# Attention queries and keys transposed unsplit and split on the way out of PSUM

## The chip, the cores and the metric

The kernel runs on one core of a Trainium2 chip. A core has five engines with queues of their own: TensorE (PE in the profile; its weight loads are PEld), VectorE (DVE), ScalarE (ACT), GpSimd (POOL) and SyncE (SP), which issues the DMAs. An engine works through its queue in order; semaphores make one wait for another. The metric is device microseconds of one execution of the whole program.

## The reference

A trunk of two layers over 2048 tokens of width 1024 in float32: a Mamba-2 layer and a layer of sliding-window attention with sinks. The change concerns the second.

```python
def swa_sink_mixer(h, cos, sin, w_in, sinks, w_out):
    q, k, v, gate = jnp.split(h @ w_in, [ATT_WIDTH, ...], axis=-1)      # 16 heads of q, 4 of k and v, 64 wide
    q = apply_partial_rope(q.reshape(b, L, ATT_Q_HEADS, D), cos, sin)   # the first 16 of 64 columns rotate
    k = apply_partial_rope(k.reshape(b, L, Hk, D), cos, sin)
    s = jnp.einsum('bnikgd,bnjkd->bnkgij', qb, kb) * (D ** -0.5)        # blocks of 128 against 256 keys
    s = jnp.where(valid, s, -jnp.inf)                                   # window of 128
    m = jnp.maximum(jnp.max(s, axis=-1, keepdims=True), sink)
    p = jnp.exp(s - m)
    denom = jnp.sum(p, axis=-1, keepdims=True) + jnp.exp(sink - m)
    o = jnp.einsum('bnkgij,bnjkd->bnikgd', p / denom, vb)
    return (o.reshape(b, L, ATT_WIDTH) * jax.nn.silu(gate)) @ w_out
```

The whole layer is x + rmsnorm(mixer(rmsnorm(x))). Float32 products are made of three F32R matmuls each: an operand is rounded to F32R (hi) and its remainder is rounded too (lo), and hi*hi + hi*lo + lo*hi are summed in PSUM (`mm3`, lines 89 to 93).

## The kernel before

The attention layer is the function `att`. It runs a loop over n of 64 iterations: two halves of the tokens, in each of them four groups of heads (kv: four heads of q, one of k and v), in each of these eight blocks of 128 tokens (i). Three more iterations empty the pipeline. `hf`, `kv` and `i` are n // 32, n // 8 % 4 and n % 8.

In one iteration n, five blocks are in work at once. `proj(n)` makes q, k and v of block n with 24 matmuls (lines 91 to 93 with operands qh, ql) and, at its end, brings them out of the PSUM tile ps: the columns that don't rotate by ScalarE (line 362), v by VectorE (line 364), the rotation by VectorE (lines 371 to 374). The result is qf, four heads of q and one of k. `stage_a(n - 1)` transposes, `stage_b(n - 2)` makes scores and softmax (lines 422 to 442), `stage_c(n - 3)` transposes the probabilities (line 450) and masks them (lines 452 and 456), and, in each second iteration, `stage_d` multiplies two blocks with v (lines 471 and 475) and writes them out. An iteration with `stage_d` is longer than one without; they alternate. Between these parts stand pieces of `proj` and of `gate_mm`, which projects the gate (lines 91 to 93 with whi, wlo; lines 347 and 348).

Before the change, the split into hi and lo is made ahead of the transposes. ScalarE rounds q (line 376), GpSimd subtracts (line 377), so that hi and lo of a head stand side by side as 128 columns; VectorE does the same for k (lines 380 and 381), with hi twice and lo twice. One transpose per head of q then gives a tile with hi in partitions 0 to 63 and lo in 64 to 127; two transposes give k as hi over hi and lo over lo. The scores of a head are two matmuls over 128 partitions (line 422), which together sum all four products.

PSUM is scarce here. The pool `tp` has a single buffer (tag "tr"), which the tiles tq (transposed q), tt (transposed probabilities) and pt (transposed x) take in turn. The pool `pp` has four (tag "pj"): the ps of projections and gates, tk (transposed k), and the u of the output projection.

At i = 0 a group of heads begins: SyncE loads its weights, ScalarE rounds them (lines 151 and 331) and GpSimd subtracts (lines 153 and 333), in tiles wraw, whi, wlo (gate) and qr, qh, ql (q, k and v).

The program is written through a tile framework, which sets the order on each engine itself by a plan made ahead of the run, and adds the semaphores. The order therefore differs from that of the code, and it changes where an edit changes the plan.

Of the kernel before, what the change touches and what calls it, by code (L numbers as in the profile page):

```python
# [11 lines left out]
F32 = mybir.dt.float32  # L12
F32R = mybir.dt.float32r
I32 = mybir.dt.int32
U32 = mybir.dt.uint32
AF = mybir.ActivationFunctionType
ALU = mybir.AluOpType
# [4 lines left out]
P = 128  # L22
# [37 lines left out]
class Trunk:  # L60
# [7 lines left out]
    def consts(self, pool):  # L68
        nc = self.nc
        self.ident = pool.tile([P, P], F32, name="ident")  # L70
        make_identity(nc, self.ident)
        self.identr = pool.tile([P, P], F32R, name="identr")
        nc.vector.tensor_copy(self.identr, self.ident)
        self.ones = pool.tile([P, P], F32, name="ones")
        nc.gpsimd.memset(self.ones, 1.0)

        self.triu = pool.tile([P, P], F32, name="triu")
        nc.gpsimd.affine_select(self.triu, self.ones, pattern=[[1, P]], compare_op=ALU.is_ge,
                                fill=0.0, base=0, channel_multiplier=-1)
        self.mhalf = pool.tile([P, 1], F32, name="mhalf")  # L80
        nc.vector.memset(self.mhalf, -0.5)
# [214 lines left out]
    def att(self, ctx, x1, oT, wn, rs1, hs0, wout, sts):  # L296
        nc, io = self.nc, self.io
        w_in = io["att_w_in"][0]
        KO, VO, GO = QW, QW + KVW, QW + 2 * KVW
        if True:  # L300
            wp = self.pool(ctx, "c_w", 2)
            cp = self.pool(ctx, "c_c")
            ap = self.pool(ctx, "c_a", 2)
# [11 lines left out]
            ksave = [cp.tile([P, 2, P], F32R, name=f"ksave{n}") for n in range(4)]  # L315
            vsave = [cp.tile([P, 64], F32, name=f"vsave{n}") for n in range(4)]
            NS = 64
            S = [dict() for _ in range(NS)]
# [31 lines left out]
            def proj(n, ws, hs):  # L350
                hf, kv, i = n // 32, n // 8 % 4, n % 8
                hi, lo = hs[i // 4]
                sl = slice((i % 4) * P, (i % 4) * P + P)
                ps = self.pp.tile([P, 6, 64], F32, tag="pj", name="ps")
                pf = ps.rearrange("p a b -> p (a b)")
                for k in range(KD):
                    wh, wl = ws[k]
                    self.mm3(pf, hi[:, k, sl], lo[:, k, sl], wh, wl, k == 0, k == KD - 1)
                    if k % 2 == 1 and k < KD - 1:
                        yield 1.0  # L360
                qf = ap.tile([P, 5, 64], F32, tag="qf", name="qf")
                nc.scalar.activation(qf[:, :, 16:64], ps[:, 0:5, 16:64], AF.Copy)
                vt = vsave[kv] if (hf == 0 and i == 7) else ap.tile([P, 64], F32, tag="vt", name="vt", bufs=6)
                nc.vector.tensor_copy(vt, ps[:, 5, :])
                ti = 8 * hf + i
                m1 = ap.tile([P, 5, 16], F32, tag="m1", name="m1")
                m2 = ap.tile([P, 5, 16], F32, tag="m2", name="m2")

                def bc(t, a, b):
                    return t[:, ti, a:b].unsqueeze(1).to_broadcast([P, 5, b - a])  # L370
                nc.vector.tensor_tensor(m1, ps[:, 0:5, 0:16], bc(self.cs2, 0, 16), ALU.mult)
                nc.vector.tensor_tensor(m2[:, :, 0:8], ps[:, 0:5, 8:16], bc(self.sn2, 0, 8), ALU.mult)
                nc.vector.tensor_tensor(m2[:, :, 8:16], ps[:, 0:5, 0:8], bc(self.sn2, 8, 16), ALU.mult)
                nc.vector.tensor_tensor(qf[:, :, 0:16], m1, m2, ALU.add)
                qs = ap.tile([P, 4, 2, 64], F32R, tag="qs", name="qs")
                nc.scalar.activation(qs[:, :, 0, :], qf[:, 0:4, :], AF.Copy)  # L376
                nc.gpsimd.tensor_tensor(qs[:, :, 1, :], qf[:, 0:4, :], qs[:, :, 0, :].bitcast(F32), ALU.subtract)  # L377
                ks = ap.tile([P, 2, 2, 64], F32R, tag="ks", name="ks")
                kb = qf[:, 4:5, :].to_broadcast([P, 2, 64])
                nc.vector.tensor_copy(ks[:, 0, :, :], kb)  # L380
                nc.vector.tensor_tensor(ks[:, 1, :, :], kb, ks[:, 0, :, :].bitcast(F32), ALU.subtract)  # L381
                S[n].update(qs=qs, ks=ks, vt=vt)

            def stage_a(n):
                hf, kv, i = n // 32, n // 8 % 4, n % 8
                qs, ks = S[n]["qs"], S[n]["ks"]
                tq = self.tp.tile([P, 4, P], F32, tag="tr", name="tq")
                for r in range(4):
                    nc.tensor.transpose(tq[:, r, :].bitcast(F32R), qs[:, r].rearrange("p a b -> p (a b)"), self.identr)  # L389
                qT = ap.tile([P, 4, P], F32R, tag="qT", name="qT")  # L390
                nc.scalar.activation(qT, tq, AF.Copy)
                tk = self.pp.tile([P, 2, P], F32, tag="pj", name="tk")
                for v in range(2):
                    nc.tensor.transpose(tk[:, v, :].bitcast(F32R), ks[:, v].rearrange("p a b -> p (a b)"), self.identr)  # L394
                if i == 0:
                    kk = ap.tile([P, 2, 2 * P], F32R, tag="kk", name="kk", bufs=3)
                    if hf == 1:
                        nc.vector.tensor_copy(kk[:, :, 0:P], ksave[kv].bitcast(F32))
                    S[n]["kk"] = kk
                kk = S[n]["kk"]  # L400
                nc.vector.tensor_copy(kk[:, :, P:2 * P], tk)
                if i < 7:
                    k2 = ap.tile([P, 2, 2 * P], F32R, tag="kk", name="kk", bufs=3)
                    nc.scalar.activation(k2[:, :, 0:P], tk, AF.Copy)
                    S[n + 1]["kk"] = k2
                elif hf == 0:
                    nc.scalar.activation(ksave[kv], tk, AF.Copy)
                S[n]["qT"] = qT

            def stage_b(n):  # L410
# [79 lines left out]
            for n in range(NS + 3):  # L490
                pr = iter(())
                if n < NS:
                    hf, kv, i = n // 32, n // 8 % 4, n % 8
                    if n == 28:
                        hs2 = []
                        pre = self.prep(x1, 2, wn, hs2, rs1)
                        next(pre)
                    if 28 <= n < 32:
                        next(pre)
                    if n == 32:  # L500
                        drain(pre)
                        hs = hs2
                    if n % 32 == 0:
                        pre = self.prep(x1, 2 * hf + 1, wn, hs, rs1)
                        next(pre)
                    if i == 0:
                        wg = [self.split_w(w_in[:, GO + 256 * kv + P * c:GO + 256 * kv + P * c + P], P)
                              for c in range(2)]
                        ws = load_qkv(kv)
                    if i % 4 == 0:  # L510
                        drain(gate)
                        gate = gate_mm(kv, i // 4, hs, wg)
                        if n % 32 == 0:
                            drain(gate)
                    if n % 32 < 4:
                        next(pre)
                    pr = proj(n, ws, hs)
# [25 lines left out]
                if n % 2 == 0:  # L543
                    lagged(stage_d, n - 3)
                lagged(stage_a, n - 1)
                part(True)
            drain(head)
# [475 lines left out]
```

## Time and profile before

| | us |
|---|---|
| median of three runs (lowest, highest) | 2607.88 (2606.68, 2608.61) |
| the profiled execution | 2604.63 |
| its span, first to last instruction | 2602.9 |
| TensorE busy | 2555.3 |
| VectorE busy | 1726.8 |
| ScalarE busy | 1264.8 |
| GpSimd busy | 1087.6 |

The mean granted clock of TensorE over the span is 0.998 of full speed. The attention loop runs from about 1780 to 2430 us of the span. The profile names an instruction by engine, line, operation and tiles (out<-in). A matmul's time contains its way through the array, so that matmuls in a row overlap: their pace is read from their starts. "L364 DVE ... [0.34 <-ACT qf L362]" says that VectorE stood idle for 0.34 us ahead of this instruction until ScalarE's line 362 released it.

### The profile page before, as it was taken

Reading aid. Unit: us, or ns where it says so; the run is one execution under the profiler, and the core shown is the slowest. Engines: PE = TensorE matmul, PEld = TensorE weight load, DVE = VectorE, ACT = ScalarE, POOL = GpSimd, SP = SyncE. Lnnn points to the kernel's source line nnn. Section 1 sums busy time; section 2 is a strip of 40 time slices with the busy share of each in tenths; the row PEclk is TensorE's granted clock in tenths of the full one; section 3 lists DMA queues with packets and bytes.
Section 4 is the critical chain, followed back from the end, with each engine's and each line's share of the span. In section 5 each row is a group of like instructions: output and inputs, shape, how many; then the busy total and the mean of one; then the engine's idle time right before and its main releaser. Section 6 shows DMA issues by size and latency. Waiting matters only on the chain. (4 is left out here: it accounts for less than half of the span.)

```text
span 2602.9 us, 39510 instructions
## 1 busy us (share of the span) xinstructions
PE 2555.3 (98%) x14307; PEld 2128.2 (82%) x14307; DVE 1726.8 (66%) x3580; ACT 1264.8 (49%) x3015; POOL 1087.6 (42%) x1013
## 2 busy tenths in 40 slices
PE   7999999999999999999998999999999999999998
PEld 6778888888777888888886888888888888888787
DVE  6678666776787667766687544447777777777422
ACT  5455555555654555555556323324455455554321
POOL 2455555655555556555566322222222122221222
PEclk9999999999999999999999999999999999999999
DMA  4332222222323222222225332234111121101343
GB/s 126 104 81 70 82 76 75 84 64 82 100 73 116 74 78 80 71 78 78 78 81 152 117 104 91 96 131 143 54 53 54 57 79 53 54 27 61 110 146 122
DMA packets 266659, 224.50 MB, mean 86 GB/s; under 512 B 31136, under 2 KB 229984, under 8 KB 266464
## 3 DMA queue, kind: packets, MB, share of 16 engines
q1 hardware_dynamic: 266464, 221.98, 27.9%
q8 instruction: 113, 1.85, 0.3%
q14 instruction: 82, 0.67, 0.1%
HBM read 179.72 MB, written 42.21 MB: 85 GB/s over the span
## 5 line engine op out<-in xcount | busy, mean ns | idle before, releaser
L91 PE MATMUL ps<-hi,whi 128*128 128x512 f32 (+1 forms) x1808 | 732.2, 405 | 1.4 <-ACT hi L140 1.0
L93 PE MATMUL ps<-hi,wlo 128*128 128x512 f32 (+1 forms) x1808 | 707.3, 391 | 0.4 <-POOL wlo L153 0.4
L92 PE MATMUL ps<-lo,whi 128*128 128x512 f32 (+1 forms) x1808 | 703.7, 389 | 0.5 <-DVE lo L141 0.5
L91 PEld LDWEIGHTS ps<-hi,whi 128*128 128x128 f32 x1808 | 341.1, 189 | 77.9 <-issue 18.8
L93 PEld LDWEIGHTS ps<-hi,wlo 128*128 128x128 f32 x1808 | 340.8, 188 | 76.4 <-POOL wlo L153 1.2
L92 PEld LDWEIGHTS ps<-lo,whi 128*128 128x128 f32 x1808 | 342.0, 189 | 57.4 <-DVE lo L141 1.3
L745 DVE SCALAR_TENSOR_TENSOR acc<-raw,cw,acc 128x512 f32<-128x512 f32 x384 | 344.0, 896 | 21.7 <-ACT acc L742 17.2
L153 POOL TENSOR_TENSOR wlo<-wraw,whi 128x1024 fp32r<-128x1024 f32 x114 | 282.6, 2479 | 173.3 <-ACT whi L151 164.7
L798 ACT ACTIVATE dec<-ab,acs 128x128 f32<-128x128 f32 x512 | 167.1, 391 | 174.0 <-DMA ab<-atd 168.1
L804 POOL TENSOR_TENSOR ab<-ab,sx 128x512 f32<-128x512 f32 x120 | 163.2, 1360 | 193.2 <-ACT ab L803 193.0
L252 PE MATMUL u<-oh,yh 128*128 128x512 f32 x768 | 241.1, 394 | 0.0
L252 PE MATMUL u<-ol,yh 128*128 128x512 f32 x768 | 239.3, 392 | 0.0
L252 PE MATMUL u<-oh,yl 128*128 128x512 f32 x768 | 237.8, 390 | 0.0
L748 ACT ACTIVATE sx<-acc 128x512 f32<-128x512 f32 x128 | 80.8, 632 | 267.0 <-DVE acc L745 266.9
L377 POOL TENSOR_TENSOR qs<-qf,qs 128x256 fp32r<-128x256 f32 x64 | 48.7, 762 | 343.5 <-ACT qs L376 306.7
L236 POOL TENSOR_TENSOR yl<-yr,yh 128x1024 fp32r<-128x1024 f32 (+1 forms) x64 | 120.5, 1883 | 160.5 <-ACT yh L234 157.9
L841 POOL TENSOR_TENSOR ysb<-ysb,zz 128x128 f32<-128x128 f32 x256 | 162.6, 648 | 49.5 <-DVE ysb L839 48.7
L91 PE MATMUL ps<-qh,hi 128*128 128x384 f32 x512 | 177.8, 348 | 0.0
L92 PE MATMUL ps<-ql,hi 128*128 128x384 f32 x512 | 173.0, 338 | 0.9 <-POOL ql L333 0.9
L93 PE MATMUL ps<-qh,lo 128*128 128x384 f32 x512 | 172.2, 337 | 0.0
L252 PEld LDWEIGHTS u<-oh,yl 128*128 128x128 f32 x768 | 144.2, 188 | 31.8 <-issue 0.6
L252 PEld LDWEIGHTS u<-ol,yh 128*128 128x128 f32 x768 | 143.8, 188 | 30.7 <-issue 0.2
(217 smaller groups left out, 4759.6 us busy)
## 6 DMA issues: line engine op xcount, KB each, us to landing
wraw<-in_ssm_w_in SPq DMA_DIRECT2D x98, 512.0 KB, 3.9
ab<-atd SPq DMA_DIRECT2D x128, 256.0 KB, 3.3
xt<-in_x SPq DMA_DIRECT2D x32, 512.0 KB, 4.9
yT<-ysb SPq DMA_DIRECT2D x64, 256.0 KB, 2.2
yr<-yT SPq DMA_DIRECT2D x32, 512.0 KB, 4.0
xt<-x SPq DMA_DIRECT2D x32, 512.0 KB, 4.1
oraw<-in_ssm_w_out SPq DMA_DIRECT2D x16, 512.0 KB, 6.1
x<-xt SPq DMA_DIRECT2D x32, 256.0 KB, 2.1
```

Source lines behind the costliest of these rows:

```text
L91: nc.tensor.matmul(ps, sh, mh, start=first, stop=False)
L92: nc.tensor.matmul(ps, sh, ml, start=False, stop=False)
L93: nc.tensor.matmul(ps, sl, mh, start=False, stop=last)
L153: nc.gpsimd.tensor_tensor(lo, raw, hi.bitcast(F32), ALU.subtract)
L236: nc.gpsimd.tensor_tensor(yl, yr, yh.bitcast(F32), ALU.subtract)
L252: nc.tensor.matmul(st["u"][h], y[:, k, :], w[:, j, 512 * h:512 * h + 512], start=k0 + k == 0 and m == 0, stop=k0 + k == kt - 1 and m == 2)
L377: nc.gpsimd.tensor_tensor(qs[:, :, 1, :], qf[:, 0:4, :], qs[:, :, 0, :].bitcast(F32), ALU.subtract)
L745: nc.vector.scalar_tensor_tensor(acc, raw[:, j:j + BLK], self.cw[:, j, ct:ct + 1], acc, ALU.mult, ALU.add)
L748: nc.scalar.activation(sx, acc, AF.Tanh)
L798: nc.scalar.activation(dec[:, r, :], ab[:, r, :], AF.Relu, scale=-1.0, bias=acs[:, c, 4 * g + r:4 * g + r + 1])
L804: nc.gpsimd.tensor_tensor(ce, ce, Ct[:, sl].unsqueeze(1).to_broadcast([P, 4, P]), ALU.mult)
L841: nc.gpsimd.tensor_tensor(yv, yv, res[f"z{pr}", s][:, sl], ALU.mult)
```

## The change

q and k are transposed as they are, and split afterwards. Two heads of q make 128 columns of qf, so two transposes give all four heads; qf gets a sixth head, a copy of k, so that a third transpose gives k twice, in partitions 0 to 63 and 64 to 127. All three go into one tile tq of the pool `tp`, and are F32 now, with the F32 identity. Out of PSUM, for each of the two heads of a pair, ScalarE rounds its 64 partitions into hi, and VectorE subtracts into the other 64 partitions of qT (lines 388 and 389 afterwards). k is rounded over all 128 partitions and subtracted likewise (lines 396 and 397). The copy of k for the next block is made by GpSimd from SBUF (lines 400 and 403), instead of by ScalarE from PSUM. The tiles qs, ks, tk and the F32R identity go. The scores (line 422, afterwards 418) are untouched. Lines from `consts` to `proj` have numbers smaller by 2 afterwards, lines behind `stage_a` smaller by 4: line 450 becomes 446, line 442 becomes 438.

```diff
-        self.identr = pool.tile([P, P], F32R, name="identr")
-        nc.vector.tensor_copy(self.identr, self.ident)
...
-                qf = ap.tile([P, 5, 64], F32, tag="qf", name="qf")
-                nc.scalar.activation(qf[:, :, 16:64], ps[:, 0:5, 16:64], AF.Copy)
+                qf = ap.tile([P, 6, 64], F32, tag="qf", name="qf")
+                nc.scalar.activation(qf[:, 0:5, 16:64], ps[:, 0:5, 16:64], AF.Copy)
...
-                nc.vector.tensor_tensor(qf[:, :, 0:16], m1, m2, ALU.add)
-                qs = ap.tile([P, 4, 2, 64], F32R, tag="qs", name="qs")
-                nc.scalar.activation(qs[:, :, 0, :], qf[:, 0:4, :], AF.Copy)
-                nc.gpsimd.tensor_tensor(qs[:, :, 1, :], qf[:, 0:4, :], qs[:, :, 0, :].bitcast(F32), ALU.subtract)
-                ks = ap.tile([P, 2, 2, 64], F32R, tag="ks", name="ks")
-                kb = qf[:, 4:5, :].to_broadcast([P, 2, 64])
-                nc.vector.tensor_copy(ks[:, 0, :, :], kb)
-                nc.vector.tensor_tensor(ks[:, 1, :, :], kb, ks[:, 0, :, :].bitcast(F32), ALU.subtract)
-                S[n].update(qs=qs, ks=ks, vt=vt)
+                nc.vector.tensor_tensor(qf[:, 0:5, 0:16], m1, m2, ALU.add)
+                nc.vector.tensor_copy(qf[:, 5, :], qf[:, 4, :])
+                S[n].update(qf=qf, vt=vt)
 
             def stage_a(n):
                 hf, kv, i = n // 32, n // 8 % 4, n % 8
-                qs, ks = S[n]["qs"], S[n]["ks"]
-                tq = self.tp.tile([P, 4, P], F32, tag="tr", name="tq")
-                for r in range(4):
-                    nc.tensor.transpose(tq[:, r, :].bitcast(F32R), qs[:, r].rearrange("p a b -> p (a b)"), self.identr)
+                qf = S[n]["qf"].rearrange("p a b -> p (a b)")
+                tq = self.tp.tile([P, 3, P], F32, tag="tr", name="tq")
+                for t in range(3):
+                    nc.tensor.transpose(tq[:, t, :], qf[:, t * P:(t + 1) * P], self.ident)
                 qT = ap.tile([P, 4, P], F32R, tag="qT", name="qT")
-                nc.scalar.activation(qT, tq, AF.Copy)
-                tk = self.pp.tile([P, 2, P], F32, tag="pj", name="tk")
-                for v in range(2):
-                    nc.tensor.transpose(tk[:, v, :].bitcast(F32R), ks[:, v].rearrange("p a b -> p (a b)"), self.identr)
+                qe = qT.rearrange("p (t e) i -> p e t i", e=2)
+                for e in range(2):
+                    rows, other = slice(64 * e, 64 * e + 64), slice(64 - 64 * e, P - 64 * e)
+                    nc.scalar.activation(qe[rows, e], tq[rows, 0:2, :], AF.Copy)
+                    nc.vector.tensor_tensor(qe[other, e], tq[rows, 0:2, :], qe[rows, e].bitcast(F32), ALU.subtract)
...
                 kk = S[n]["kk"]
-                nc.vector.tensor_copy(kk[:, :, P:2 * P], tk)
+                nc.scalar.activation(kk[:, 0, P:2 * P], tq[:, 2, :], AF.Copy)
+                nc.vector.tensor_tensor(kk[:, 1, P:2 * P], tq[:, 2, :], kk[:, 0, P:2 * P].bitcast(F32), ALU.subtract)
                 if i < 7:
                     k2 = ap.tile([P, 2, 2 * P], F32R, tag="kk", name="kk", bufs=3)
-                    nc.scalar.activation(k2[:, :, 0:P], tk, AF.Copy)
+                    nc.gpsimd.tensor_copy(k2[:, :, 0:P], kk[:, :, P:2 * P].bitcast(F32))
                     S[n + 1]["kk"] = k2
                 elif hf == 0:
-                    nc.scalar.activation(ksave[kv], tk, AF.Copy)
+                    nc.gpsimd.tensor_copy(ksave[kv], kk[:, :, P:2 * P].bitcast(F32))
```

The plan moves with it. TensorE's queue at the start of the loop, where n = 1 begins: before,

```order
L91 MATMUL ps<-qh,hi 128x384
L92 MATMUL ps<-ql,hi 128x384
L93 MATMUL ps<-qh,lo 128x384
L394 MATMUL tk<-identr,ks 128x128
L137 MATMUL pt<-ident,xt 128x128 x3
L389 MATMUL tq<-identr,qs 128x128 x4
L394 MATMUL tk<-identr,ks 128x128
L137 MATMUL pt<-ident,xt 128x128
```

and now, with lines 135 and 383 for the transposes of x and of qf:

```order
L89 MATMUL ps<-qh,hi 128x384
L90 MATMUL ps<-ql,hi 128x384
L91 MATMUL ps<-qh,lo 128x384
L135 MATMUL pt<-ident,xt 128x128 x4
L89 MATMUL ps<-qh,hi 128x384
L90 MATMUL ps<-ql,hi 128x384
L91 MATMUL ps<-qh,lo 128x384
L89 MATMUL ps<-qh,hi 128x384
L90 MATMUL ps<-ql,hi 128x384
L91 MATMUL ps<-qh,lo 128x384
L89 MATMUL ps<-qh,hi 128x384
L90 MATMUL ps<-ql,hi 128x384
```

The first transposes of the loop have moved behind the transposes of x and nine projection matmuls.

VectorE's queue in a short iteration of the second half of the tokens, from the sum of the row maxima on: before,

```order
L440 TENSOR_TENSOR ds<-ds,es 128x4
L401 CAST kk<-tk 128x2x128
L441 RECIPROCAL ds<-ds 128x4
L442 TENSOR_TENSOR s<-s,ds 128x512
L364 COPY vt<-ps 128x64
```

and now, where line 389 subtracts q, line 397 subtracts k and line 373 copies k within qf:

```order
L436 TENSOR_TENSOR ds<-ds,es 128x4
L437 RECIPROCAL ds<-ds 128x4
L389 TENSOR_TENSOR qT<-tq,qT 64x2x128
L438 TENSOR_TENSOR s<-s,ds 128x512
L389 TENSOR_TENSOR qT<-tq,qT 64x2x128
L362 COPY vt<-ps 128x64
L369 TENSOR_TENSOR m_22199<-ps,cs_96 128x80
L370 TENSOR_TENSOR m_22200<-ps,sn_97 128x5x8
L371 TENSOR_TENSOR m_22200<-ps,sn_97 128x5x8
L397 TENSOR_TENSOR kk<-tq,kk 128x128
L372 TENSOR_TENSOR qf<-m_22199,m_22200 128x5x16
L346 SCALAR_TENSOR_TENSOR zz<-zz,ps 128x512
```

The copy out of tk stood ahead of line 442; the last reader of tq stands behind it and behind the first steps of the next block's rotation.

ScalarE's queue in the iteration in which a new group's weights are rounded, from the first exponential on: before,

```order
L438 ACTIVATE s,ds<-s,nm 128x128
L435 ACTIVATE es<-es 128x4
L438 ACTIVATE s,ds<-s,nm 128x128 x3
L331 ACTIVATE qh<-qr 128x384
L391 ACTIVATE qT<-tq 128x512
L404 ACTIVATE kk<-tk 128x2x128
L331 ACTIVATE qh<-qr 128x384
L362 ACTIVATE qf<-ps 128x5x48
L151 ACTIVATE whi<-wraw 128x1024
```

and now, with lines 388 (q) and 396 (k) for the copies out of tq:

```order
L434 ACTIVATE s,ds<-s,nm 128x128 x3
L329 ACTIVATE qh<-qr 128x384
L388 ACTIVATE qT<-tq 64x2x128
L329 ACTIVATE qh<-qr 128x384
L360 ACTIVATE qf<-ps 128x5x48
L329 ACTIVATE qh<-qr 128x384
L388 ACTIVATE qT<-tq 64x2x128
L149 ACTIVATE whi<-wraw 128x1024
L396 ACTIVATE kk<-tq 128x128
```

The last reader of tq on this engine stands behind the rounding of a gate weight, where the copies of q and k stood ahead of it.

## Rows read from the trace of the kernel before

**Rows 1.** The page's busy time by engine: us (share of span) xinstructions.

```profile
PE 2555.3 (98%) x14307; PEld 2128.2 (82%) x14307; DVE 1726.8 (66%) x3580; ACT 1264.8 (49%) x3015; POOL 1087.6 (42%) x1013
```

**Rows 2.** Busy time by stretch; columns PE, PEld, DVE, ACT, POOL, PEclk, DMA.

```profile
1792.50:1796.50 4.00, 3.89 (x19) 3.79 (x20) 2.88 (x6) 2.66 (x6) 1.72 (x3) 0.57 0.26 71
2170.00:2250.00 80.00, 80.00 (x505) 70.59 (x504) 58.07 (x156) 40.40 (x135) 18.99 (x19) 1.00 0.17 49
```

**Rows 3.** Timeline of TensorE, one short iteration: start us, us, instruction, count.

```profile
2209.91 0.46 PE L389 MATMUL tq<-identr,qs 128*128 128x128 f32 x4
...
2210.62 0.34 PE L92 MATMUL ps<-ql,hi 128*128 128x384 f32 x1
...
2213.91 0.60 PE L450 MATMUL tt<-ident,s 128*128 128x128 f32 x4
```

**Rows 4.** Timeline of TensorE at the start of the loop, F32 transposes.

```profile
1782.21 0.38 PE L137 MATMUL pt<-ident,xt 128*128 128x128 f32 x2
...
1782.79 0.60 PE L137 MATMUL pt<-ident,xt 128*128 128x128 f32 x4
...
1783.40 0.34 PE L92 MATMUL ps<-ql,hi 128*128 128x384 f32 x1
```

**Rows 5.** Waits in 1792 to 2440: us in total, times, longest.

```profile
PEld ps L91 <- ACT kk L404: 1.8, 6, 0.7
```

**Rows 6.** Timeline of TensorE at n = 1.

```profile
1791.68 0.25 PE L394 MATMUL tk<-identr,ks 128*128 128x128 f32 x1 [1.24 <-DVE m L372]
```

**Rows 7.** Instructions on the tile ks: duration ns min/median/max, first and last start.

```profile
L380 DVE CAST ks<-qf x64: 214/227/2322, 1791.3 to 2413.4; 128x128 fp32r<-128x128 f32 x64
L381 DVE TENSOR_TENSOR ks<-qf,ks x64: 274/293/2461, 1791.6 to 2415.2; 128x128 fp32r<-128x128 f32 x64
```

**Rows 8.** Groups by form on VectorE: count | busy us, mean ns | idle before.

```profile
L401 DVE CAST kk<-tk 128x256 fp32r<-128x256 f32 x64 | 26.8, 419 | 3.7 <-PE tk L394 3.2
L781 DVE TENSOR_TENSOR xd<-pt,dt 128x256 f32<-128x256 f32 x128 | 53.4, 417 | 34.8 <-PE pt L777 33.6 <-PE yt L829 0.7
L793 DVE TENSOR_TENSOR bl<-pt,bh 128x128 fp32r<-128x128 f32 x128 | 36.7, 287 | 84.6 <-ACT bh L791 84.6
```

**Rows 9.** Groups by form on ScalarE.

```profile
L404 ACT ACTIVATE kk<-tk 128x256 fp32r<-128x256 f32 x56 | 21.2, 379 | 18.7 <-DVE kk L401 17.8
L791 ACT ACTIVATE bh<-pt 128x128 fp32r<-128x128 f32 x128 | 33.2, 259 | 0.0
```

**Rows 10.** Group by form on GpSimd, the subtraction of q.

```profile
L377 POOL TENSOR_TENSOR qs<-qf,qs 128x256 fp32r<-128x256 f32 x64 | 48.7, 762 | 343.5 <-ACT qs L376 306.7 <-PE tt L450 30.8 <-PE sc L422 6.0
```

**Rows 11.** Timeline of the iteration of rows 3, VectorE and ScalarE.

```profile
2210.39 0.16 DVE L440 TENSOR_TENSOR ds<-ds,es 128x4 f32<-128x4 f32 x1 [1.62 <-ACT s L438]
2211.12 0.69 DVE L442 TENSOR_TENSOR s<-s,ds 128x512 f32<-128x512 f32 x1
2212.15 0.23 DVE L364 COPY vt<-ps 128x64 f32<-128x64 f32 x1 [0.34 <-ACT qf L362]
2212.38 0.60 ACT L347 ACTIVATE zz<-ps 128x512 f32<-128x512 f32 x1 [0.26 <-PE ps L93]
2212.55 0.19 DVE L373 TENSOR_TENSOR m<-ps,sn 128x40 f32<-128x40 f32 x1
```

**Rows 12.** Timeline where a gate weight is split, GpSimd beside VectorE.

```profile
2153.84 2.40 POOL L153 TENSOR_TENSOR wlo<-wraw,whi 128x1024 fp32r<-128x1024 f32 x1 [7.74 <-ACT whi L151]
2153.93 2.46 DVE L381 TENSOR_TENSOR ks<-qf,ks 128x128 fp32r<-128x128 f32 x1
```

**Rows 13.** Timeline of the end of an iteration at a group's boundary.

```profile
2172.13 0.51 ACT L331 ACTIVATE qh<-qr 128x384 fp32r<-128x384 f32 x1
2172.25 0.16 DVE L440 TENSOR_TENSOR ds<-ds,es 128x4 f32<-128x4 f32 x1 [1.62 <-ACT s L438]
2173.95 1.05 ACT L151 ACTIVATE whi<-wraw 128x1024 fp32r<-128x1024 f32 x1
2174.34 0.65 PE L450 MATMUL tt<-ident,s 128*128 128x128 f32 x4
```

## The prediction

> **What bounds the kernel now.** I read the page first: TensorE is busy for 98% of the span [rows 1]. Then the table by stretches: in the attention stage, which the change alone touches, TensorE is busy in all of 80 us, while VectorE is busy for 58 and ScalarE for 40 [rows 2]. So TensorE's stream of matmuls sets the time there, and VectorE is near enough behind it to matter: a VectorE busy for 73% that also waits for the exponentials once in each iteration has little left over. Next comes the timeline of one iteration of the loop over n. It starts at the transposes of line 450, and the next ones start at 2213.91, after the six transposes of lines 389 and 394 and four groups of projections [rows 3]. Nothing stands idle in it. A change is therefore worth what it takes out of TensorE's stream, minus what TensorE has to wait afterwards.
>
> **What goes out of TensorE's stream.** 64 iterations lose six transposes in F32R and get three in F32. Before, the first of the six starts at 2209.91, and the second matmul behind them (it is the first that starts at its usual pace) at 2210.62: 0.71 us [rows 3]. F32 transposes of the same shape stand in line 137: four of them start at 1782.79, and the second matmul behind starts at 1783.40, which is 0.61; two take 0.38 and four 0.60, so one more costs 0.11 [rows 4]. Three then cost 0.61 - 0.11 = 0.50, and an iteration gets shorter by 0.21. 64 x 0.21 = 13.4 us. If the three took as long as the six, this would be zero; the pace of line 137 is the same operation and shape, so I take 13.4.
>
> The tile tk goes, and with it a buffer of the four that projections, gates and tk share. Weight loads of line 91 waited 1.8 us for ScalarE's copy out of tk [rows 5]; part of that is hidden by the matmul ahead, so I take 1.0.
>
> **The start of the stage.** At n = 1 TensorE stood idle for 1.24 us, because the first transpose of tk waited for VectorE [rows 6]. In the stretch behind it the granted clock was 0.57, so part of these 4 us ran at the lower of the two levels, 1.2 GHz [rows 2]: about 4.0 x 0.43 = 1.7 us lost. In the new order nine projection matmuls stand where that wait was. Against that, the first scores now follow a longer chain. Between 0 and 2.9 saved; I take 1.5.
>
> **What the other engines get.** VectorE loses the two ks operations (medians 0.227 and 0.293 [rows 7]) and the copy out of tk (0.419 [rows 8]), 0.94 together. It gets two subtractions from PSUM over 256 columns, for which line 781 is nearest (0.417), one over 128 columns like line 793 (0.287) [rows 8], and a copy of 64 columns, at most the 0.227 of line 380; I take 0.2. Half the partitions need not be half the time, so I give the subtractions the full 0.417. That is 1.32, so 0.38 more per iteration. ScalarE gets two copies of 256 columns (0.379 each, line 404) and one of 128 (0.259, line 791) [rows 9], for one copy of 512, one of 256 and the rounding of qs; it does no more than before. GpSimd's subtraction qs (0.762 [rows 10]) goes, and a copy of the keys comes, which is not shown in the trace: between nothing and that 0.762. Nobody waits for it within an iteration.
>
> **What is late next.** All six readers of the new tq take turns: copy, subtract, copy, subtract for the two halves of q, then copy and subtract for k. tq is the single buffer of its pool, and the transposes of line 450 write the next tile in it. So these transposes, which waited for line 442 alone, now also wait for the last subtraction of k. Behind them in TensorE's queue stands everything. I walk one short iteration (one without the products of lines 471 and 475) with [rows 11]. The sum of the row maxima (line 440) starts at 2210.39. The three transposes end near 2210.4, the first copy 0.38 later at 2210.8, the first subtraction at 2211.2; line 442 takes 0.69, to 2211.9; the second copy ran meanwhile, the second subtraction ends at 2212.3. Then vt and the three rotation products, which took from 2212.15 to 2212.74, end at 2212.9. ScalarE's copy of k stands behind the gate's tanh (2212.38 to 2212.98 before, 0.21 earlier now), so it ends near 2213.0, and k's subtraction at about 2213.3. TensorE gets to line 450 at 2213.91 - 0.21 = 2213.70. It is on time with some 0.3 us to spare, where line 442 used to end 2.1 us ahead. In the first half of the sequence some iterations put the subtraction of k behind zz or the rotation's sum; these come 0.2 late. Cost in ordinary iterations: 1 to 3 us in all, I take 2.
>
> The spare time is gone where a new group of heads begins, seven times. There GpSimd splits new weights, and VectorE operations between SBUF operands are held up: a subtraction ks of 0.293 took 2.46 us from 2153.93, beside a GpSimd split of 2.40 us from 2153.84 [rows 12]. The Trainium skill (SBUF — State Buffer, section "SBUF: two separate sides") says that the two engines share a port pair as an exclusive lock for a whole instruction, and that VectorE wants it in a two-port mode or with two SBUF inputs; the trace agrees with 2.46 beside 2.40. By that rule the new subtractions, which read one operand from PSUM, are not exposed, and the 64-column copy is.
>
> Before, such a delay ate into the 2.1 us. Now it reaches TensorE. ScalarE's queue is the second cause: in the iteration that ends with line 450 at 2174.34, its last exponential ended just before 2172.25 [rows 13]. In the new order three roundings of qh (0.51 each), the copies of q (2 x 0.38), the eviction of qf (as line 404, 0.38) and the rounding of a gate weight (1.05) stand ahead of the copy of k (0.26) and its subtraction (0.29): 4.27 by durations, 3.5 if each overlaps its neighbour by 0.1. That gives 2175.7 to 2176.5, against 2174.13 when TensorE is there: 1.6 to 2.4 late. But VectorE was itself late by 1.4 there (line 440 starts 2.09 us ahead of line 450, against 3.52 in [rows 11]); without that lateness it is 0.2 to 1.0. TensorE has some 0.4 us of scores and projections that the new order puts ahead of line 450. I take 0.9 for this iteration, and 0.25 for the one before, which meets the first of the weight splits: 1.15 x 7 = 8 us, between 2 and 20.
>
> **The sum**, against the profiled execution's own 2604.63: - 13.4 - 1.0 - 1.5 + 2 + 8 = - 5.9, so 2598.7. The median of the runs shown, 2607.88, is 3.25 above the profiled execution, so the forecast for a median is 2602.0. The boundaries are its softest term.
>
> **Rivals.**
> 1. *Clean gain.* Boundaries cost 2 and the ordinary iterations nothing: 13.4 + 1.0 + 2.5 - 2 = 15 faster, 2593. For it: fewer VectorE operations between SBUF operands are left to be held up. The port rule of the Trainium skill, taken alone, says this. Against it: the 0.3 us of spare time. Chance 0.20.
> 2. *Stalls eat the gain.* 2.5 us at each of seven boundaries and 3 in the others: 20.5 against 15.9, so 4.6 slower, 2612.5; with 2.0 at a boundary 2609, with 3.0 2616. For it: the upper walk of [rows 13]. Chance 0.20.
> 3. *VectorE becomes the bound.* The copy of 64 columns and the rotation's sum are held up by GpSimd's new copy of the keys in each iteration, and the subtraction of k ends after 2213.70 in the 32 short ones. At 0.6 late each this is 19 on top of the 8 + 2, against 15.9: 13 slower, 2621. This is the case on the other side. It decides as soon as k's subtraction ends over 0.3 us later than walked. Against it: the wait for the exponentials (1.6 us) and the longer iterations give VectorE time to catch up. Chance 0.12.
> 4. *The transposes give nothing.* Three in F32 cost what six in F32R did: - 5.9 + 13.4 = + 7.5, 2615. Against it: [rows 4]. Chance 0.03.
> 5. The forecast, between 2596 and 2609: chance 0.45.
>
> **How the numbers follow.** About 0.2% (5.2 us) is what a measurement of this kernel can tell from no change. Faster than 2602.7: all of rival 1 and half of the forecast, 0.20 + 0.23 = 0.43. Slower than 2613.1: half of rival 2, rivals 3 and 4, 0.10 + 0.12 + 0.03 = 0.25. Between: 0.32. The range from 2591 to 2616 leaves out rival 3, part of rival 4 and the outer end of rival 1. The forecast's own range is 2596 to 2609.
>
> **What would show it.** Three transposes of tq and the second matmul behind them in 0.50 us; 0.21 us less between two transposes of line 450 (line 446 afterwards) in an ordinary iteration. No idle at n = 1 and no low clock there. TensorE's waits name VectorE's subtraction into kk ahead of line 446, mostly around the splits of new weights, with 5 to 12 us in sum; under 3 is rival 1, over 15 rival 2, and waits in every short iteration are rival 3. Wrong would be a wait on GpSimd's copy of the keys that reaches TensorE, or an attention stage with VectorE busy without breaks.

## The result, and the profile after

The changed kernel is slower: 2625.55 us (2624.35 to 2630.97, four runs) against 2607.28 (2605.97 to 2608.61), ratio 1.0076 (95% interval 1.0061 to 1.0091). I had forecast 2602.0, with a range to 2616. The profiled execution took 2624.35 us, 19.7 more than that of before.

First the page's busy times, for [rows 1], and the same stretches as in [rows 2], with one stretch more.

```profile
PE 2556.1 (97%) x14115; PEld 2117.7 (81%) x14115; DVE 1738.5 (66%) x3643; ACT 1253.6 (48%) x3019; POOL 1063.5 (41%) x1009
```

```profile
1792.50:1796.50 4.00, 4.00 (x27) 3.92 (x26) 2.71 (x13) 1.96 (x5) 0.00 (x0) 1.00 0.79 191
2170.00:2250.00 80.00, 76.71 (x468) 67.02 (x467) 59.38 (x162) 38.59 (x134) 15.79 (x17) 1.00 0.17 47
2352.00:2355.40 3.40, 3.40 (x16) 3.21 (x15) 1.78 (x5) 0.77 (x2) 0.37 (x1) 0.50 0.22 61
```

TensorE was busy in all of the 80 us before; now 3.3 us are missing in them, and 468 matmul records stand where there were 505, of which some 24 are the transposes that went (three in each of eight iterations). VectorE has hardly more to do (59.4 for 58.1). So it is not a lack of throughput: something makes TensorE wait. The table of TensorE's waits (1790 to 2460; in total, times, longest) says for what.

```profile
PE tt L446 <- DVE qf L373: 10.4, 6, 2.2
PE sc L418 <- ACT kk L396: 9.6, 14, 3.3
PE tt L446 <- DVE lo L139: 1.1, 1, 1.1
```

The ordinary iterations did what the sum said. Timeline of TensorE for the three transposes, beside [rows 3], and the transposes of line 446 at the two ends of a long iteration:

```profile
1907.13 0.49 PE L383 MATMUL tq<-ident,qf 128*128 128x128 f32 x3
1907.38 0.42 PE L89 MATMUL ps<-qh,hi 128*128 128x384 f32 x1
1907.64 0.34 PE L90 MATMUL ps<-ql,hi 128*128 128x384 f32 x1
...
2206.23 0.60 PE L446 MATMUL tt<-ident,s 128*128 128x128 f32 x4
...
2216.90 0.60 PE L446 MATMUL tt<-ident,s 128*128 128x128 f32 x4
```

From the first transpose to the second matmul behind it are 0.51 us (0.50 forecast), and an ordinary pair of iterations takes 8.65 + 10.67 = 19.32, where it took 8.86 + 10.89 = 19.75: 0.21 less for each.

The loss is at the boundaries. The first of the two waits, in the iteration in which GpSimd splits the first gate weight of a new group:

```profile
1910.38 2.36 POOL L151 TENSOR_TENSOR wlo<-wraw,whi 128x1024 fp32r<-128x1024 f32 x1 [8.35 <-ACT whi L149]
...
1910.49 2.35 DVE L372 TENSOR_TENSOR qf<-m,m 128x80 f32<-128x80 f32 x1
1912.76 0.28 DVE L397 TENSOR_TENSOR kk<-tq,kk 128x128 fp32r<-128x128 f32 x1
...
1912.96 0.18 DVE L373 COPY qf<-qf 128x64 f32<-128x64 f32 x1
...
1913.19 0.63 PE L446 MATMUL tt<-ident,s 128*128 128x128 f32 x4 [2.10 <-DVE qf L373]
```

The rotation's sum (line 372) reads and writes SBUF. It takes 0.29 us at the median and 2.35 here, beside GpSimd's 2.36. Behind it in VectorE's queue stands k's subtraction (line 397), the last reader of tq, and line 446 needs that buffer: TensorE idles for 2.10 us, where some 0.3 were to spare. The profile names line 373, which merely ended last; tq isn't read by it: in all six of these waits line 446 starts 0.146 or 0.147 us after the end of line 397, while the end of line 373 lies 0.03 to 0.05 us ahead. Four of the six are of 2.1 us, one in each of four boundaries; the other two are of 0.7 and 1.2.

The second wait comes two iterations later and has another cause:

```profile
1931.25 0.51 ACT L329 ACTIVATE qh<-qr 128x384 fp32r<-128x384 f32 x1
...
1931.79 0.38 ACT L388 ACTIVATE qT<-tq 64x256 fp32r<-64x256 f32 x1
...
1932.19 1.06 ACT L149 ACTIVATE whi<-wraw 128x1024 fp32r<-128x1024 f32 x1
...
1933.28 0.28 ACT L396 ACTIVATE kk<-tq 128x128 fp32r<-128x128 f32 x1
...
1933.70 0.48 PE L418 MATMUL sc<-kk,qT 128*128 128x256 f32 x2 [1.00 <-ACT kk L396]
```

ScalarE rounds q's and the gate's new weights ahead of k's copy, and the plan has put two scores, which need that copy, ahead of line 446. This is the queue that I walked with [rows 13]. ScalarE isn't late by its own roundings alone, however. GpSimd splits q's new weights too (line 331), and while it does, VectorE's line 430, a subtraction with two SBUF operands that takes 0.16 us at the median, takes 0.92; ScalarE's exponentials idle for 0.45 behind it:

```profile
1926.61 1.98 POOL L331 TENSOR_TENSOR ql<-qr,qh 128x384 fp32r<-128x384 f32 x2 [1.47 <-ACT qh L329]
...
1927.69 0.92 DVE L430 TENSOR_TENSOR es<-nm,nsink 128x4 f32<-128x4 f32 x1
...
1928.64 0.20 ACT L431 ACTIVATE es<-es 128x4 f32<-128x4 f32 x1 [0.45 <-DVE es L430]
```

Once both causes met: at 2348 the copy of 64 columns was held for 2.22 us with q's second subtraction behind it, TensorE idled for 3.26, and in the stretch from 2352.0 the granted clock was 0.50 of full speed, its level of 1.2 GHz: another 1.7 us.

```profile
2348.24 2.22 DVE L373 COPY qf<-qf 128x64 f32<-128x64 f32 x1
2350.49 0.43 DVE L389 TENSOR_TENSOR qT<-tq,qT 64x256 fp32r<-64x256 f32 x1
...
2351.43 0.48 PE L418 MATMUL sc<-kk,qT 128*128 128x256 f32 x2 [3.26 <-ACT kk L396]
```

A ledger of the stage shows where to look further. The stretches run between the starts of the first matmul with operands qh and lo (line 93 before, 91 afterwards) in iterations 0, 8, 28 and 40, and of the last one of iteration 63. TensorE transposes x for the second half of the tokens in iterations 27 to 35, nearly all of it in the third stretch (56 of 64 transposes before, 60 now).

| stretch (us) | 0 to 8 | 8 to 28 | 28 to 40 | 40 to 63 | sum |
|---|---|---|---|---|---|
| before | 68.0 | 199.3 | 125.8 | 237.2 | 630.2 |
| changed | 67.7 | 201.9 | 131.5 | 245.0 | 646.1 |

The stage is 15.9 us longer, the work behind it 0.8. The other 3.1 lie ahead of the stage, where TensorE does the same work in both kernels: in the fourteen profiles of this study that part took from 1779.7 to 1786.4, and the kernel before was at the low end. In the medians both kernels share that scatter.

### The profile page after: what moved, and what is told of

It is laid out like the page before. It is cut to its first block, busy times and chain, and to the rows that moved or that the text cites. A ratio compares the mean times of both kernels' runs of the same rounds, so it can differ in the third digit from the quotient of the medians.

```text
span 2622.6 us, 39276 instructions
## 1 busy us (share of the span) xinstructions
PE 2556.1 (97%) x14115; PEld 2117.7 (81%) x14115; DVE 1738.5 (66%) x3643; ACT 1253.6 (48%) x3019; POOL 1063.5 (41%) x1009
## 5 line engine op out<-in xcount | busy, mean ns | idle before, releaser
L232 ACT ACTIVATE yh<-yr 128x1024 fp32r<-128x1024 f32 (+1 forms) x64 | 54.1, 845 | 237.3 <-PE u L250 176.0
```

The source lines that it names most:

```text
L232: nc.scalar.activation(yh, yr, AF.Copy)
```

## The experiments

Theory A: VectorE's operations between SBUF operands are held by GpSimd's splits, and k's subtraction stands behind them. Theory B: ScalarE's roundings hold up the copies out of tq. Theory D: VectorE has too much work in any iteration. Each kernel was timed in five rounds beside the kernel before, whose median was 2607.62, 2607.24 and 2607.79 in the three sets of four; ratios are to it.

**Small splits.** In `split_w`, for the attention alone:

```diff
-        nc.gpsimd.tensor_tensor(lo, raw, hi.bitcast(F32), ALU.subtract)
+        for j in range(0, kt, kt // parts): nc.gpsimd.tensor_tensor(lo[:, j:j + kt // parts], raw[:, j:j + kt // parts], hi[:, j:j + kt // parts].bitcast(F32), ALU.subtract)
```

(`parts` is 4 for the gate's weights; the splits of the weights of q, k and v, line 331, stay whole.)

> The changed kernel, but GpSimd subtracts each gate weight of the attention in four pieces of 256 columns instead of one of 1024; the order on TensorE, VectorE and ScalarE stays what it was. Theory A (VectorE's operations between SBUF operands, the rotation's sum and the copy of k, are held for the length of GpSimd's subtraction, and k's subtraction, the last reader of tq, stands behind them): a held operation takes at most about 0.8 us instead of 2.4, the six waits of line 446 (10.4 us) fall under 2, the wait of 3.3 at 2351 falls under 2; 2610 to 2615. Theory B (ScalarE's roundings of weights ahead of k's copy are what makes tq late): nothing or up to 3 less, 2622 to 2626. Theory D (VectorE has too much work): 2624 to 2627.

Measured: 2615.22, ratio 1.0033 (1.0021 to 1.0045), 10 us better than the changed kernel. TensorE's waits (1790 to 2440) are now

```profile
PE sc L418 <- ACT kk L396: 7.9, 14, 1.6
PE tt L446 <- DVE kk L397: 2.3, 5, 0.5
PE pt L135 <- DVE kk L397: 2.2, 1, 2.2
```

The 10.4 of line 446 have become 2.3, under their right name. The order on TensorE, VectorE and ScalarE is that of the changed kernel, so this much is A. The waits for ScalarE stay. The wait of 2.2 for transposes of x is new (at 2084.95), and 3.4 us at 1.2 GHz follow it (from 2086.4).

**A sum that reads PSUM.** The product with the cosine goes back to PSUM:

```diff
-                nc.vector.tensor_tensor(m1, ps[:, 0:5, 0:16], bc(self.cs2, 0, 16), ALU.mult)
...
-                nc.vector.tensor_tensor(qf[:, 0:5, 0:16], m1, m2, ALU.add)
+                nc.vector.tensor_tensor(ps[:, 0:5, 0:16], ps[:, 0:5, 0:16], bc(self.cs2, 0, 16), ALU.mult)
+                nc.vector.tensor_tensor(qf[:, 0:5, 0:16], ps[:, 0:5, 0:16], m2, ALU.add)
```

> The changed kernel, with the product of the rotation's cosine written back to PSUM, so that the rotation's sum reads one operand from PSUM; the copy of 64 columns is as it was. Theory A with only operations between SBUF operands held: the sum takes 0.25 to 0.35 us beside GpSimd's subtraction, not 2.4, the waits of line 446 behind it go, the wait of 3.3 at 2351 (behind the copy) may stay: 2611 to 2617. If operations that read PSUM are held as well, or by theory B: 2622 to 2627.

Measured: 2614.23, ratio 1.0024 (1.0015 to 1.0032). The sum's durations (min/median/max) in the changed kernel and in this one, and this one's copy of 64 columns:

```profile
L372 DVE TENSOR_TENSOR qf<-m,m x64: 230/288/2414, 1794.1 to 2432.3; 128x80 f32<-128x80 f32 x64
```

```profile
L372 DVE TENSOR_TENSOR qf<-ps,m x64: 227/241/243, 1796.9 to 2423.7; 128x80 f32<-128x80 f32 x64
L373 DVE COPY qf<-qf x64: 182/195/1847, 1797.2 to 2425.0; 128x64 f32<-128x64 f32 x64
```

With one operand in PSUM not one of 64 sums is held, though 45 of them began while GpSimd was at work; the copy between SBUF operands still is. So it is the sum's second SBUF operand that exposes it. The Trainium skill (SBUF — State Buffer, section "SBUF: two separate sides") states that an operation of VectorE with two inputs in SBUF, or in a two-port mode, and an operation of GpSimd that reads SBUF lock each other out; for the sum the trace agrees, 0.243 at most against 2.414. Theory A's "operations between SBUF operands" is too wide, however. In the changed kernel the row maximum (line 425), with one operand in SBUF and its result there, began ten times while GpSimd was at work and was never held, unlike line 430 with its two:

```profile
L425 DVE TENSOR_REDUCE mx<-s x64: 627/686/689, 1801.9 to 2447.4; 128x4 f32<-128x512 f32 x64
```

```profile
L430 DVE TENSOR_TENSOR es<-nm,nsink x64: 154/163/945, 1803.3 to 2449.1; 128x4 f32<-128x4 f32 x64
```

The plan moved with this edit (short iterations of the second half take 8.96 us instead of 8.65), so the 11 us gained are not the sum's alone.

**k first.** In `stage_a`, the two lines that read k out of tq are written ahead of the loop that reads q:

```diff
+                nc.scalar.activation(kk[:, 0, P:2 * P], tq[:, 2, :], AF.Copy)
+                nc.vector.tensor_tensor(kk[:, 1, P:2 * P], tq[:, 2, :], kk[:, 0, P:2 * P].bitcast(F32), ALU.subtract)
                 qT = ap.tile([P, 4, P], F32R, tag="qT", name="qT")
...
-                nc.scalar.activation(kk[:, 0, P:2 * P], tq[:, 2, :], AF.Copy)
-                nc.vector.tensor_tensor(kk[:, 1, P:2 * P], tq[:, 2, :], kk[:, 0, P:2 * P].bitcast(F32), ALU.subtract)
```

> The changed kernel, with k's copy and subtraction written ahead of those of q, so that the last reader of tq is the second subtraction of q, which the plan puts ahead of the next block's rotation. Theory A: the waits of line 446 behind the rotation's sum go (10 us), and the scores no longer wait for k's copy behind a gate weight (10 us): 2603 to 2609. Theory B: q's second copy takes the place of k's behind the roundings, half is left: 2612 to 2620. Theory D: 2624 to 2627.

Measured: 2616.52, ratio 1.0030 (1.0020 to 1.0041). A alone is refuted; the time is in theory B's range. q's second copy now stands behind the gate weight's rounding, q's second subtraction behind the next rotation, and the waits bear its name (line 397 in this kernel; longest 3.4 us):

```profile
PE tt L446 <- DVE qT L397: 9.4, 9, 3.4
PE sc L418 <- DVE qT L397: 2.5, 5, 0.9
```

**k first, with small splits** (both edits).

> k_first, with GpSimd's gate weights subtracted in four pieces; the order on TensorE, VectorE and ScalarE is that of k_first. Theories A and B together: the waits behind held operations go (3.4 us at 2267, 1.5 at 2163), those behind ScalarE's rounding of a gate weight, which stands ahead of q's second copy, stay (1.0 us at each boundary): 2604 to 2609. A alone: 2600 to 2603. Theory B alone: 2615 to 2618.

Measured: 2612.96, ratio 1.0023 (1.0014 to 1.0032). That lies between the ranges that I named: less came back than I expected. Line 446 still waits for q's second subtraction, 1.27 us at the worst. ScalarE's rounding is ahead of that subtraction's operand, but held operations are a part of it here too: at 2180.03 the copy of 64 columns, ahead of it on VectorE, takes 0.88 us beside a split of q's weights of 1.03 (line 331), which the edit leaves whole. TensorE then runs 3.4 us at 1.2 GHz twice (from 2181.9 and 2263.8). Whichever reader comes last, it stands behind something at a boundary.

**k in a tile of its own.** tq holds q alone; the third transpose goes to a tile of the pool of four, as before the change:

```diff
-                tq = self.tp.tile([P, 3, P], F32, tag="tr", name="tq")
+                tq, tk = self.tp.tile([P, 2, P], F32, tag="tr", name="tq"), self.pp.tile([P, P], F32, tag="pj", name="tk")
```

(The third transpose and the two lines that read k are changed to match.)

> The changed kernel, with the third transpose (k) in a tile of its own from the pool of four, as before the change; tq holds q alone. Theory A: line 446 no longer waits for k's subtraction (10 us less, and 1 to 2 more for the buffer of the pool), the scores still wait for k's copy: 2612 to 2617. Theory B and D: 2622 to 2627, with line 446 waiting for q's second subtraction instead.

Measured: 2606.71, ratio 0.9992 (0.9983 to 1.0000): better than any theory said, 19 us better than the changed kernel. The stretches are 67.5, 195.7, 126.2 and 238.0. The middle, 131.5 in the changed kernel, is back near what it was (125.8). The plan moved a good deal with this edit: in the iteration of the second wait the changed kernel has two scores between the transposes of q and line 446, and here there are none. So the 19 us belong to the tile and to the order that came with it, and no run separates the two. What is left at a boundary is A again, one step removed:

```profile
2177.27 2.40 POOL L151 TENSOR_TENSOR wlo<-wraw,whi 128x1024 fp32r<-128x1024 f32 x1
...
2177.44 2.28 DVE L373 COPY qf<-qf 128x64 f32<-128x64 f32 x1
...
2187.52 0.42 DVE L389 TENSOR_TENSOR qT<-tq,qT 64x256 fp32r<-64x256 f32 x1
...
2188.09 0.63 PE L446 MATMUL tt<-ident,s 128*128 128x128 f32 x4 [1.13 <-DVE qT L389]
```

The held copy makes VectorE's softmax late, and with it q's last subtraction ten microseconds on.

**k in its own tile, with small splits** (both edits).

> k_own_tile, with GpSimd's gate weights subtracted in four pieces as in small_splits; the order on TensorE, VectorE and ScalarE is that of k_own_tile. There the three iterations at a boundary took 9.36, 11.96 and 8.84 us, against 8.66, 10.68 and 8.66 elsewhere: 2.2 us at a boundary, 15 in all. Theory A (a held copy of k makes the next softmax late, and with it the copies of q): half to three quarters of it goes, 2596 to 2600. Theory B (ScalarE's roundings): 2604 to 2607.

Measured: 2598.47, ratio 0.9964 (0.9952 to 0.9977). The order on TensorE, VectorE and ScalarE is that of k in its own tile, so these 8 us are A. This version beats both kernels, by 8.8 and by 27 us. Of TensorE's waits of line 446 for q's last subtraction 0.2 us are left. The stretches: 67.1, 194.9, 124.7, 232.8.

**One set of weights**, in the changed kernel and in the kernel before:

```diff
-                    if i == 0:
+                    if n == 0:
                         wg = [self.split_w(w_in[:, GO + 256 * kv + P * c:GO + 256 * kv + P * c + P], P)
```

> The changed kernel, but all groups of heads use the weights of the first, so that no weights are loaded, rounded or subtracted at the seven later boundaries (the attention's result is then that of other weights). If the work on new weights is the whole of the loss (A and B together): 2590 to 2598, with all short iterations near 8.65 and all long ones near 10.67. If VectorE has too much work in any iteration (D): 2610 or more.

> The kernel before, with the same omission: all groups use the weights of the first. All theories: the work at the boundaries was hidden before, so 2603 to 2607; the distance to a_one_weights is the gain of the change without its stalls, 11 to 16 us if the terms of the sum for TensorE and the start were right.

Measured: 2600.04, ratio 0.9970 (0.9958 to 0.9982), and 2604.54, ratio 0.9992 (0.9983 to 1.0000). The first is 2 above the range of A and B together, and far under theory D's, which falls. New weights cost the changed kernel 25.5 us and the kernel before 2.7. But the distance between the two is 4.5 and not 11 to 16. Their stretches are 66.7, 193.3, 128.8, 232.1 and 69.0, 197.4, 125.0, 236.5: outside the middle the change gains 10.8, of which 8.5 in the 44 iterations from 8 to 28 and from 40 on; in the middle it loses 3.8, where 12 x 0.21 = 2.5 should have been gained: 6.3 in all. Some 0.4 of the 6.3 is no stall: four transposes of x more stand in this stretch (60 for 56, at 0.11 each by [rows 4]). TensorE's rows with idle time there (1.6 us in all, from 2046 to 2175) are of two kinds:

```profile
2080.41 0.63 PE L135 MATMUL pt<-ident,xt 128*128 128x128 f32 x4 [0.18 <-DVE kk L397]
...
2110.65 0.47 PE L418 MATMUL sc<-kk,qT 128*128 128x256 f32 x2 [0.32 <-ACT kk L396]
```

The four transposes of x that use the single buffer wait until k is read out of tq, and scores that the plan put ahead of them wait for k's copy. The kernel before has no such wait there. The idle rows show less than the starts do, since matmuls overlap. Counted by starts, the first scores behind a projection come 2.5 us late in sum in these twelve iterations (0.57 us from the projection's start instead of 0.17, and the like), the transposes of x 0.8 late, and in the kernel before neither: the larger share is the scores that wait for k's copy. Some 2.6 of the 6.3 I can't lay to single rows. Whether the shared buffer is behind it the next kernel is to show.

**tq in the pool of four, with small splits:**

```diff
-                tq = self.tp.tile([P, 3, P], F32, tag="tr", name="tq")
+                tq = self.pp.tile([P, 3, P], F32, tag="pj", name="tq")
```

> small_splits, with tq taken from the pool of four instead of the pool with a single buffer, so that neither the transposes of the probabilities nor those of x wait for any reader of tq. If the shared single buffer is what costs (boundaries, and 6 us in the twelve iterations in the middle where x is transposed): 2597 to 2604. If ScalarE's roundings reach TensorE by the scores as well, which need k's copy: 2605 to 2612.

Measured: 2611.13, ratio 1.0013 (1.0004 to 1.0022), in the second range. The middle took 125.0 (132.6 with small splits alone), so the shared buffer is the likely cause of the loss in the middle; k in its own tile (126.2, and 124.7 with small splits) points the same way. Both edits move the plan as well, and fewer scores stand ahead of line 446 there, so that the buffer is not shown to be the cause by itself. But now the gate's matmuls wait for a buffer of their pool, behind k's copy and the rotation of the block before, and ordinary short iterations take 9.10 instead of 8.65:

```profile
2220.53 0.19 PEld L89 LDWEIGHTS ps<-hi,whi 128*128 128x128 f32 x1 [0.50 <-ACT kk L396]
2220.56 0.47 PE L89 MATMUL ps<-hi,whi 128*128 128x512 f32 x1 [0.21 <-DVE m L371]
```

**Rounding on GpSimd.** In the attention's `split_w` GpSimd rounds too, piece by piece; once on small splits, once on k in its own tile with small splits:

```diff
-        nc.scalar.activation(hi, raw, AF.Copy)
+        if parts == 1: nc.scalar.activation(hi, raw, AF.Copy)
```

(GpSimd's copy into hi then stands in the loop of the pieces, ahead of each subtraction.)

> small_splits, with the attention's gate weights rounded by GpSimd as well, in the same four pieces, so that ScalarE has one operation of 1.05 us less ahead of k's copy at each boundary; GpSimd has some 1.6 us more for each weight. Theory B (ScalarE's queue holds up k's copy, which the scores and line 446 wait for): 2605 to 2611. If it is GpSimd's work alone that counts: 2614 to 2618.

> own_small, with the gate weights rounded by GpSimd too. What is left at a boundary there is 0.1, 0.3 and 0.2 us in three iterations, 4 in all: by theory B 2595 to 2598. If ScalarE's queue no longer matters once k has its own tile: 2598 to 2600.

Measured: 2612.30, ratio 1.0015 (1.0006 to 1.0024), and 2602.10, ratio 0.9979 (0.9970 to 0.9989). The first outcome lies between the two that I named, 2.9 better than small splits; its longest wait of a score for k's copy is 0.8 instead of 1.6. The gate's rounding is a part of B, not the whole: a boundary's four iterations take 8.65, 10.67, 10.27 and 10.29 us instead of 9.30, 10.70, 10.58 and 10.29, so that 0.3 went from the second wait, and 0.65 from the first, which in small splits was a wait for VectorE's held operations and not for ScalarE. The second is 3.6 worse: with k in its own tile the gate's rounding on ScalarE no longer reaches TensorE at a boundary (8.77, 10.94 and 8.83 us before and after this edit), and in its profile the stage's start and middle are longer, the middle with a stretch at 1.2 GHz.

**Small splits in the kernel before.**

> The kernel before, with GpSimd's gate weights subtracted in four pieces as in small_splits. With one set of weights it came down by 2.7 us only, so there is hardly anything to get back: 2604 to 2608. If the pieces were a gain by themselves, whatever the transposes: 2595 to 2600.

Measured: 2604.28, ratio 0.9989 (0.9980 to 0.9998). So 3.5 us of the best version's 8.8 belong to the pieces, which the kernel before can have as well, and 5.3 to the unsplit transposes with k in its own tile.

## Why the prediction was wrong, point by point

- **TensorE's stream**: right. 0.50 was 0.51, and 0.21 less for an iteration is what ordinary iterations show. Six transposes did not cost what three do (rival 4).
- **Costs of the new operations**: right. q's subtractions take 0.422 (0.417 taken), k's 0.282 (0.287), the copy of 64 columns 0.195 (0.2), ScalarE's copies 0.379 and 0.277. Half the partitions are not half the time.
- **The walk of an ordinary iteration**: right. In the short one that starts at 2216.90 k's subtraction ends 0.28 us ahead of line 446; 0.3 was forecast. The 2 us set aside for late ones were not needed.
- **The start**: the idle 1.24 and the low clock are gone [rows 2, 6], but line 418 idles for 0.46 there and line 383 for 0.57. Of the 1.5 forecast 0.6 came: without new weights, the first eight iterations gain 2.3, of which 1.7 is the transposes.
- **The boundaries**: the step that failed. "I take 0.9 for this iteration, and 0.25 for the one before": 8 in all. Measured: 25.5 - 2.7 = 22.8. An ordinary boundary's iterations take 10.97, 10.69, 10.58 and 10.28 us instead of 8.66, 10.67, 8.66 and 10.67. So the second cause costs 1.92 less the 0.39 given back, 1.5 for 0.9 forecast; the first costs 2.3, not 0.25. (The seven boundaries are not alike; their mean is 22.8 / 7 = 3.3.) I had read in [rows 12] that an operation between SBUF operands is held for 2.4 us, and that k's subtraction sometimes stands behind the rotation's sum, and charged "these come 0.2 late", the sum's own duration. The two belong together: the sum is an operation between SBUF operands, and at the boundary it is the one that is held. I applied the port rule to the operations that were added, and not to one that stood there already and had become the one ahead of the release. How the second cause divides between ScalarE's roundings and held operations (lines 430 and 373 beside line 331) stays open: no run cut the splits of line 331.
- **The middle**: not in the sum at all, as if it cost nothing; 6.3 us (3.8 lost and 2.5 not gained). tq shares its buffer with x's transposes too, and the plan put scores ahead of line 446 there; which of the two costs more stays open.
- **The rivals**: stalls that eat the gain (rival 2) was the right mechanism with too low a price: 2612.5 at 2.5 for a boundary, 3.3 were paid, and the middle came on top. Rival 3 had nearly the time (2621) and the wrong reason. GpSimd's copy of the keys does hold the rotation's sum (0.31 to 0.40 us instead of 0.23 in 16 of 64 cases of the changed kernel with one set of weights), but ordinary iterations are none the longer for it (8.65 and 10.67).

With the measured sizes the sum is - 13.4 (transposes) - 0.6 (start) + 22.8 (boundaries) + 6.3 (middle) = + 15.1, against 15.9 in the stage. That is bookkeeping and not a proof, since two terms are differences of the same kernels. The gain of the transposes was real in ordinary iterations. With k in its own tile and small splits about half of it shows in the stage: 619.5 us, 6.9 less than the kernel before with small splits.

## What to carry to other kernels

Before a tile in a single buffer gets more readers, list for its last reader what stands ahead of it on its engine in the worst iteration, not in the ordinary one, and price each of these at its longest duration in the trace: an average iteration with 0.3 us to spare hid one that was 2.1 late. An operation that was harmless as long as nobody waited behind it keeps its price when the order changes. And a change that is good by itself may need a second one to show it: the same transposes lost 18 us with k in the shared buffer, were even with the kernel before with k in a tile of its own, and gained 5 beyond what the pieces gave once those were added.

## What the runs showed of the hardware

A VectorE sum of 128x80 with both operands in SBUF took up to 2.414 us beside GpSimd subtractions of 128x1024 (changed kernel); with one operand in PSUM it took 0.243 at most in 64 cases. A copy of 128x64 within SBUF took up to 2.216, and a subtraction of only 128x4 with two SBUF operands up to 0.945; a row maximum of 128x512 with one was not held (0.689 at most in 64 cases). Four pieces of 128x256 in place of one subtraction shortened the sum's longest to 0.841 and the copy's to 0.896. After an idle time of 3.26 us TensorE ran 3.4 us at 1.2 GHz in the changed kernel, after 2.24 us in that with small splits, and after 1.27 us in that with k first and small splits; after the four waits of 2.1 us in the changed kernel it did not.
